# Grouping the up projection's matmuls by width, and starting stationary tiles at multiples of 64 bytes

## The chip, the cores and the metric

The kernel runs on one core of one Trainium2 chip. The metric is the device time of one execution in microseconds (us), median of several runs.

## The reference

A two-layer decoder trunk on a sequence of 256 tokens with a model width of 2048, all in float32. Layer 0 mixes tokens with a top-k latent attention and a sliding-window attention, layer 1 with a forgetting attention. After its mixer each layer does the same two things:

```python
x = x + conv_ffn(rms_norm(x, ffn_norm[i]), w_up[i], ffn_conv[i], w_down[i])
gate = jax.nn.sigmoid(rms_norm(x, ple_norm[i]) @ w_ple_gate[i])
x = x + gate * (p[i] @ w_ple_proj[i])

def conv_ffn(h, w_up, conv_w, w_down):
    u = h @ w_up                      # (256, 2048) @ (2048, 2 * 5504)
    u = causal depthwise conv of width 3 over the tokens (u, conv_w)
    gate, up = jnp.split(u, 2, axis=-1)
    return (jax.nn.silu(gate) * up) @ w_down   # (256, 5504) @ (5504, 2048)
```

The up projection `h @ w_up` is the place of the change.

## The kernel before, in words

**Precision.** Most products are made from float32 operands that are split in two float32r parts, a high part (a rounding copy) and a low part (what is left). A product is the sum of three: high by high, high by low, low by high.

**Weights.** `granule` (L105) hands out 128 rows by some columns of a weight matrix in several k tiles. One DMA on SP's queue brings 1 MB (as a rule) into a `raw` buffer (three of them, L100). Each half of it is then split: ScalarE casts it into a `whi` buffer (L114) and VectorE subtracts into a `wlo` buffer (L115). There are five `whi` and five `wlo` buffers, each for one half of a granule; a buffer comes free when the last matmul that reads it has run.

**The order of the work.** The program is written in one order, and a planner of the framework lays it out on the engines' queues with its own estimate of times. It can put an instruction ahead of earlier ones on the same queue; `tc.high_priority` moves whole sections forward.

**The up projection** (L821 to L838). The 43 blocks of 128 columns are done in two parts of 22 and 21, two blocks (z = 0, 1) at a time, once for the gate half and once for the up half (`base`). Each block accumulates in a PSUM bank of its own. For each of two granules of 8 k tiles (256 columns wide), and for each k, and for each z, two matmuls follow each other: the high part of the weights is stationary and both parts of `h` move past it (512 columns, L835), then the low part of the weights is stationary and the high part of `h` moves (256 columns, L837). Per layer that are 43 x 2 x 16 = 1376 such pairs, in both layers 2752, or 5504 matmuls; 88 granules a layer, 176 in all (168 of 1 MB; the last pass of the second part has one block alone, so that 8 are half as wide).

**Behind it.** ScalarE and VectorE take a finished bank, scale it, make the convolution and the gating (L842 to L856), and split the result into `ghi` and `glo` (L859, L860), one tile for each pass `f` in the part. Those tiles are stationary in **the down projection**, which follows each part (L866 to L869): for four times 512 columns, each k tile of the part is met three times in each half of the tokens (ghi with whi, ghi with wlo, glo with whi), all at 512 columns (L142). That are 43 x 3 x 2 x 4 = 1032 matmuls a layer, 2064 in all.

**Where tiles lie.** The pool `ff` of the feed-forward stage holds, in the order in which they are first asked for: `ghi0` and `glo0` (they serve the per-layer input first, as `pT_hi` and `pT_lo`), then `cw` with 3 x 86 float32 values, 1032 bytes in each partition, then `cr`, `rb`, `u`, `un`, `sg` and the other `ghi` and `glo`, each a multiple of 512 bytes. The allocator rounds a tile's size up to 32 bytes. In the program that results, `ghi0` and `glo0` begin at a multiple of 64 bytes, and every other `ghi` and `glo` begins 32 bytes past one. `whi`, `wlo` and the normed inputs (`nf`, `np`, `n`, `y`, `yc`) begin at a multiple of 64.

Of the kernel before, what the change touches and what calls it, by code (L numbers as in the profile page):

```python
# [9 lines left out]
F32 = mybir.dt.float32  # L10
# [6 lines left out]
P = 128  # L17
S = 256
# [7 lines left out]
H_C = 32  # L26
# [5 lines left out]
NFB = D_FF // P  # L32
PLE = 256
NB = 32
RV = 384
NEG = -1e30
MAXNEG = -3.0e38
CAUSAL = -1.0e37
PR = 300
HR = 6  # L40
UP_BANKS = ("mm", "qk")
MAGIC = float(0x5F3759DF)
# [4 lines left out]
def trunk(ctx, tc, t, onehot, out):  # L47
    nc = tc.nc
# [186 lines left out]
    def attention(pool, heads, b, qk, logits, vv, y_out, halves, extra=0, mask=None):  # L235

        nh = len(heads)
        n = P * (b + 1)
        nk = n // P
        o = psum("o")  # L240
        nl = sm.tile([P, 8], F32, tag="att_l", name="att_l", bufs=2)[:, :nh]
        rl = sm.tile([P, 8], F32, tag="att_r", name="att_r", bufs=2)[:, :nh]

        def front(grps):
            per = len(grps[0])
            pss = [psum("qk") for _ in grps]
            ss = [pool.tile([P, 516], F32, tag="att_s", name="att_s", bufs=4)[:, :per * (n + extra)]
                  .rearrange("p (h c) -> p h c", h=per) for _ in grps]

            for g, i, m in alternate(grps):  # L250
                pairs = qk(heads[m], b, n)
                for c, (lt, rh) in enumerate(pairs):
                    nc.tensor.matmul(pss[g][:, i * n:(i + 1) * n], lt, rh, start=c == 0, stop=c == len(pairs) - 1)  # L253
            for grp, ps, s in zip(grps, pss, ss):
                for i, m in enumerate(grp):
                    logits(s[:, i, :], ps[:, i * n:(i + 1) * n], heads[m], b, n)
                if mask is not None:
                    nc.vector.tensor_tensor(s[:, :, :n], s[:, :, :n], mask[:, None, :n].to_broadcast([P, per, n]), op=ALU.add)
                nm = sm.tile([P, 4], F32, tag="att_m", name="att_m", bufs=4)[:, :per]
                nc.vector.tensor_reduce(nm, s, axis=AX.X, op=ALU.max, negate=True)  # L260
                for i, m in enumerate(grp):
                    nc.scalar.activation(s[:, i, :], s[:, i, :], AF.Exp, bias=nm[:, i:i + 1],
                                         accum_out=nl[:, m:m + 1])
            lo, hi = min(min(g) for g in grps), max(max(g) for g in grps) + 1
            nc.vector.reciprocal(rl[:, lo:hi], nl[:, lo:hi])
            for grp, s in zip(grps, ss):
                for i, m in enumerate(grp):
                    nc.vector.tensor_scalar(s[:, i, :n], s[:, i, :n], rl[:, m:m + 1], None, op0=ALU.mult)
            return ss

        def back(grps, ss):
            per = len(grps[0])
            pTs = []
            for s in ss:
                pt = psum()
                for i in range(per):
                    for kb in range(nk):
                        nc.tensor.transpose(pt[:, (i * nk + kb) * P:(i * nk + kb + 1) * P],  # L278
                                            s[:, i, kb * P:(kb + 1) * P], ident)
                pT = pool.tile([P, 512], F32, tag="att_p", name="att_p", bufs=2)  # L280
                nc.scalar.copy(pT[:, :per * n], pt[:, :per * n])
                pTs.append(pT)

            at = {m: (g, i) for g, i, m in alternate(grps)}
            for m in sorted(at):
                if m % 2:
                    continue
                for kb in range(nk):
                    for mm in (m, m + 1):
                        g, i = at[mm]  # L290
                        z = (mm % 2) * HD
                        nc.tensor.matmul(o[z:z + HD, m // 2 * P:(m // 2 + 1) * P], vv(heads[mm], kb),  # L292
                                         pTs[g][:, (i * nk + kb) * P:(i * nk + kb + 1) * P],
                                         start=kb == 0, stop=kb == nk - 1, skip_group_check=True)

        prev = None
        for grps in head_groups(nh, n, halves):
            ss = front(grps)
            if prev is not None:
                back(*prev)  # L300
            prev = grps, ss
        back(*prev)
        nc.vector.tensor_copy(y_out, o[:, :nh * HD])
# [29 lines left out]
    def even_mixer(i, e):  # L333
        W = t["w_in_even"][e]
        with ExitStack() as es:
            ev = es.enter_context(tc.tile_pool(name="ev", bufs=1))
# [21 lines left out]
            h = norm(t["attn_norm"][i], "n0", gains)  # L358
# [10 lines left out]
            ss = sm.tile([P, NT, 1], F32, tag="ssq", name="ssq")  # L369
# [26 lines left out]
            for m in range(2):  # L396
                pr = psum()
                nc.tensor.matmul(pr[:16, :RV], tab[:, m * 16:(m + 1) * 16], oh[:, m, :], start=True, stop=True)
                rv = ev.tile([P, 516], F32, tag="att_s", name="rv", bufs=4)[:16, :RV]
                nc.scalar.copy(rv, pr[:16, :RV])  # L400
                nc.gpsimd.dma_start(rvd[m * 16:(m + 1) * 16, :], rv)


            qg_col = ev.tile([P, 2], F32, name="qg_col")
            nc.sync.dma_start(qg_col, t["a_q_norm"][e].rearrange("(k p) -> p k", p=P))
            kvT = ev.tile([P, 2, S], F32, name="kvT")
            kvgT = ev.tile([P, 2, S], F32, name="kvgT")
# [5 lines left out]
            ss = sm.tile([P, NT, 1], F32, tag="ssq", name="ssq")  # L413
# [30 lines left out]
            for c in range(2):  # L444
                hi, lo = granule(Wqi, 0, 4, c * 512, 512)
                for f in range(0, 4, 2):
                    pq = psum()
                    for ff in range(2):
                        cols = slice((f + ff) * P, (f + ff + 1) * P)
                        for k in range(4):  # L450
                            for m, (l, r) in enumerate(((hi, cq.hi), (hi, cq.lo), (lo, cq.hi))):
                                nc.tensor.matmul(pq[:, ff * S:(ff + 1) * S], l[k][:, cols], r[:, k, :],  # L452
                                                 start=k == 0 and m == 0, stop=k == 3 and m == 2)
# [24 lines left out]
            with tc.high_priority(offset=PR):  # L478
                for b in range(NT):
                    n = P * (b + 1)  # L480
# [5 lines left out]
                    for grps in head_groups(IDX_H, n, True):  # L486
                        pds = [psum("qk") for _ in grps]
                        for g, m, hh in alternate(grps):
                            q0 = (hh % 2) * HD
                            nc.tensor.matmul(pds[g][:, m * n:(m + 1) * n], qiT[hh // 8][q0:q0 + HD, (hh % 8) // 2, b * P:(b + 1) * P],  # L490
                                             kiT[q0:q0 + HD, :n], start=True, stop=True)
                        for grp, pd in zip(grps, pds):
                            rl = ev.tile([P, 516], F32, tag="att_s", name="relu", bufs=4)[:, :512]
                            nc.scalar.activation(rl, pd, AF.Relu)
                            for m, hh in enumerate(grp):
                                nc.vector.scalar_tensor_tensor(acc[:, :n], rl[:, m * n:(m + 1) * n],
                                                               wix[b][:, hh:hh + 1], acc[:, :n],
                                                               op0=ALU.mult, op1=ALU.add)
                    m8 = ev.tile([P, 8], F32, tag="m8", name="m8", bufs=2)
                    for _ in range(TOPK // 8):  # L500
                        nc.vector.max(m8, acc[:, :n])
                        nc.vector.match_replace(acc[:, :n], m8, acc[:, :n], MAXNEG)
# [4 lines left out]

            o5 = Q_LORA + KV_LORA + HD + IDX_H + H_B * HD
            ps = moving(W, o5, 4 * HD, h.lhs, KD)
            bg = ev.tile([P, 2], F32, name="bg")  # L510
            for m, nm in enumerate(("b_q_norm", "b_k_norm")):
                for z in range(2):
                    nc.sync.dma_start(bg[z * HD:(z + 1) * HD, m:m + 1], t[nm][e].rearrange("(d o) -> d o", o=1))
# [119 lines left out]
    def odd_mixer(i, o):  # L633
        W = t["w_in_odd"][o]
        HDC = H_C * HD
        with ExitStack() as es:
            od = es.enter_context(tc.tile_pool(name="od", bufs=1))
            h = norm(t["attn_norm"][i], "n1")
            rx = h.rstd
            cg = od.tile([P, 2], F32, name="cg")  # L640
            for m, nm in enumerate(("c_q_norm", "c_k_norm")):
                for zz in range(2):
                    nc.sync.dma_start(cg[zz * HD:(zz + 1) * HD, m:m + 1], t[nm][o].rearrange("(d o) -> d o", o=1))
# [70 lines left out]

            q0 = proj_q(0)

            fb = od.tile([H_C, 1], F32, name="fb")
            nc.sync.dma_start(fb, t["c_forget_bias"][o].rearrange("(d o) -> d o", o=1))
            hi, lo = granule(W, 0, KD, 3 * HDC, H_C)
            pf = psum()  # L720
# [80 lines left out]
    def ffn(i):  # L801
        with ExitStack() as es:
# [2 lines left out]
            with tc.high_priority(offset=PR):  # L805
                h = norm(t["ffn_norm"][i], "nf")

            cw = ff.tile([P, 3, 2 * NFB], F32, name="cw")
            cr = ff.tile([2 * NFB, 3, P], F32, name="cr")
            nc.sync.dma_start(cr, t["ffn_conv"][i].rearrange("w (f c) -> f w c", c=P))  # L810
            pt = psum()
# [8 lines left out]
            for part in parts:  # L820
                g_hi, g_lo = {}, {}  # L821
                f = 0
                while f < len(part):
# [3 lines left out]
                    for base in (0, NFB):  # L827

                        pu = [psum(next(up_banks)) for _ in range(nf)]
                        for k0 in (0, 8):  # L830
                            hi, lo = granule(t["w_up"][i], k0, 8, (base + fb0) * P, nf * P)
                            for k in range(8):
                                for z in range(nf):
                                    cols = slice(z * P, (z + 1) * P)
                                    nc.tensor.matmul(pu[z], hi[k][:, cols], h.both(k0 + k), start=k0 + k == 0,  # L835
                                                     stop=k0 + k == KD - 1, skip_group_check=True)
                                    nc.tensor.matmul(pu[z][:, :S], lo[k][:, cols], h.rhs(k0 + k)[0], start=False,  # L837
                                                     stop=k0 + k == KD - 1, skip_group_check=True)  # L838
                        u = ff.tile([P, 2, S], F32, tag="u", name="u", bufs=4)
                        un = ff.tile([P, 2, S], F32, tag="un", name="un", bufs=2)  # L840
# [106 lines left out]
```

## Time and profile before

| what | value |
|---|---|
| median of 3 runs | 2449.73 us (2448.8 to 2452.66) |
| the profiled execution | 2451.84 us, span 2450.1 us, mean granted clock 0.996 |
| TensorE matmul busy | 2426.1 us of the span, 12530 matmuls |
| TensorE weight loads | 2019.7 us |
| VectorE busy | 1687.4 us |
| ScalarE busy | 1266.4 us |
| DMA | 454.25 MB, mean 185 GB/s |

A share of busy time is an average over stages. For matmuls it says little of how near the engine is to its best, since matmuls are pipelined: a matmul's recorded length is longer than the distance from its start to the next one's start. What a matmul costs here is that distance.

### The profile page before, as it was taken

To read this page: it belongs to the slowest core of one execution; us is meant where nothing else is said; L and a number is where in the kernel's file an instruction comes from. 1 tells how busy PE (TensorE), PEld (TensorE's weight loads), DVE (VectorE), ACT (ScalarE), POOL (GpSimd) and SP (SyncE) were. 2 spreads that over 40 slices of the span, in tenths; PEclk is the share of its full clock that TensorE was granted. 3 is DMA by queue.
4 is the path that set the end of the run, shared out by engine and by line. 5 is a ranking of instruction groups with operands and counts; after the bars stand their busy time and mean duration, and the time that the engine had idled before them with its cause. 6 is when DMAs were issued, how large, how long until landed. Compare 5 with 4: busy or idle time off the path is not lost.

```text
span 2450.1 us, 32617 instructions
## 1 busy us (share of the span) xinstructions
PE 2426.1 (99%) x12530; PEld 2019.7 (82%) x12530; DVE 1687.4 (69%) x2670; ACT 1266.4 (52%) x1977; POOL 63.1 (3%) x138
## 2 busy tenths in 40 slices
PE   8999999999999999999999999999999999999999
PEld 6778788888888888888778777888888888888887
DVE  7777976777546777556676777677776457776564
ACT  6556655555335555444555555465554345554443
POOL 0000100000000000000030110000000000000000
PEclk9999999999999999999999999999999999999999
DMA  8444457555556655656565555475665566655564
GB/s 275 132 139 149 143 173 233 183 184 188 179 188 200 189 183 175 198 184 225 168 215 164 180 181 176 162 240 184 184 188 180 188 199 188 184 184 187 189 197 160
DMA packets 334000, 454.25 MB, mean 185 GB/s; under 512 B 15807, under 2 KB 210019, under 8 KB 333844
## 3 DMA queue, kind: packets, MB, share of 16 engines
q1 hardware_dynamic: 332468, 447.89, 57.4%
q0 software_dynamic: 1376, 4.28, 0.5%
q8 instruction: 98, 1.61, 0.3%
q14 instruction: 58, 0.48, 0.1%
HBM read 445.76 MB, written 6.37 MB: 185 GB/s over the span
## 4 chain that ended last, share of the span: by engine, by line
PE 90%; issue 7%; DVE 1%; DMA 1%; ACT 0%; POOL 0%; DVEq 0%; SPq 0%; POOLq 0%; ACTq 0%
PE ps_mm L142 44%; PE ps_mm L835 13%; PE ps_qk L835 13%; PE ps_mm L837 7%; PE ps_qk L837 7%; PE ps_qk L253 2%; PE ps_o L292 1%; PE ps_ax L278 1%; PE ps_ax L209 1%; PE ps_ax L169 1%; PE ps_ax L452 0%; DMA pled<-y 0%; PE ps_qk L490 0%; DMA gain<-in_attn_norm_dram 0%; DVE wlo L115 0%
## 5 line engine op out<-in xcount | busy, mean ns | idle before, releaser
L115 DVE TENSOR_TENSOR wlo<-raw,whi 128x1024 fp32r<-128x1024 f32 (+1 forms) x846 | 984.8, 1169 | 611.0 <-ACT whi L114 601.7
L114 ACT CAST whi<-raw 128x1024 fp32r<-128x1024 f32 (+1 forms) x846 | 848.4, 1006 | 855.3 <-PE ps_mm L142 514.0
L835 PE MATMUL ps_qk<-nf,whi 128*128 128x512 f32 x1376 | 546.9, 399 | 0.9 <-ACT whi L114 0.9
L835 PE MATMUL ps_mm<-nf,whi 128*128 128x512 f32 x1376 | 546.4, 399 | 0.4 <-ACT y L797 0.4
L837 PE MATMUL ps_qk<-nf,wlo 128*128 128x256 f32 x1376 | 386.9, 281 | 0.9 <-DVE wlo L115 0.9
L837 PE MATMUL ps_mm<-nf,wlo 128*128 128x256 f32 x1376 | 386.7, 281 | 0.0
L142 PE MATMUL ps_mm<-whi,n 128*128 128x512 f32 (+2 forms) x1088 | 335.9, 387 | 2.4 <-ACT n L121 1.9
L835 PEld LDWEIGHTS ps_qk<-nf,whi 128*128 128x128 f32 x1376 | 258.6, 188 | 65.5 <-ACT whi L114 1.6
L835 PEld LDWEIGHTS ps_mm<-nf,whi 128*128 128x128 f32 x1376 | 258.7, 188 | 65.2 <-ACT y L797 1.1
L142 PE MATMUL ps_mm<-whi,glo 128*128 128x512 f32 x688 | 272.2, 396 | 0.0
L142 PE MATMUL ps_mm<-wlo,ghi 128*128 128x512 f32 x688 | 271.7, 395 | 0.0
L142 PE MATMUL ps_mm<-whi,ghi 128*128 128x512 f32 x688 | 271.0, 396 | 0.0
L837 PEld LDWEIGHTS ps_qk<-nf,wlo 128*128 128x128 f32 x1376 | 260.1, 189 | 2.2 <-DVE wlo L115 1.9
L837 PEld LDWEIGHTS ps_mm<-nf,wlo 128*128 128x128 f32 x1376 | 260.0, 189 | 0.1
L142 PEld LDWEIGHTS ps_mm<-whi,n 128*128 128x128 f32 x1088 | 201.7, 190 | 46.1 <-issue 6.7
L142 PE MATMUL ps_mm<-wlo,n 128*128 128x512 f32 (+2 forms) x544 | 211.0, 389 | 0.0
L142 PE MATMUL ps_mm<-whi,np 128*128 128x512 f32 x512 | 158.7, 390 | 0.0
L142 PEld LDWEIGHTS ps_mm<-wlo,ghi 128*128 128x128 f32 x688 | 129.3, 188 | 31.0
L142 PEld LDWEIGHTS ps_mm<-whi,glo 128*128 128x128 f32 x688 | 129.3, 188 | 30.7
L142 PEld LDWEIGHTS ps_mm<-whi,ghi 128*128 128x128 f32 x688 | 129.0, 188 | 30.4
L142 PEld LDWEIGHTS ps_mm<-wlo,n 128*128 128x128 f32 x544 | 103.3, 190 | 20.4 <-issue 1.4
L142 PEld LDWEIGHTS ps_mm<-whi,np 128*128 128x128 f32 x512 | 96.0, 188 | 19.8
(215 smaller groups left out, 2470.0 us busy)
## 6 DMA issues: line engine op xcount, KB each, us to landing
raw<-in_w_up_dram SPq DMA_DIRECT2D x168, 1024.0 KB, 5.3
raw<-in_w_down_dram SPq DMA_DIRECT2D x80, 1024.0 KB, 5.1
raw<-in_w_in_odd_dram SPq DMA_DIRECT2D x48, 1024.0 KB, 5.1
raw<-in_w_ple_gate_dram SPq DMA_DIRECT2D x32, 1024.0 KB, 5.2
raw<-in_w_out_even_dram SPq DMA_DIRECT2D x16, 1024.0 KB, 5.1
raw<-in_w_out_odd_dram SPq DMA_DIRECT2D x16, 1024.0 KB, 5.1
raw<-in_a_w_uq_dram SPq DMA_DIRECT2D x8, 1024.0 KB, 5.4
raw<-in_w_in_even_dram SPq DMA_DIRECT2D x8, 1024.0 KB, 5.4
```

Source lines behind the costliest of these rows:

```text
L114: nc.scalar.copy(hi, v[:, z:z + m])
L115: nc.vector.tensor_tensor(lo, v[:, z:z + m], hi.bitcast(F32), op=ALU.subtract)
L142: nc.tensor.matmul(self.ps[b], l, r[i], start=self.n[b] == 0, stop=self.n[b] == 3 * self.total - 1)
L169: nc.tensor.transpose(pt[:, i * P:(i + 1) * P], src[:, i * P:(i + 1) * P], ident)
L209: nc.tensor.transpose(pt[:, i * parts:(i + 1) * parts], src[:, i * P:(i + 1) * P], ident[:parts, :parts])
L253: nc.tensor.matmul(pss[g][:, i * n:(i + 1) * n], lt, rh, start=c == 0, stop=c == len(pairs) - 1)
L278: nc.tensor.transpose(pt[:, (i * nk + kb) * P:(i * nk + kb + 1) * P], s[:, i, kb * P:(kb + 1) * P], ident)
L292: nc.tensor.matmul(o[z:z + HD, m // 2 * P:(m // 2 + 1) * P], vv(heads[mm], kb), pTs[g][:, (i * nk + kb) * P:(i * nk + kb + 1) * P], start= ...
L835: nc.tensor.matmul(pu[z], hi[k][:, cols], h.both(k0 + k), start=k0 + k == 0, stop=k0 + k == KD - 1, skip_group_check=True)
L837: nc.tensor.matmul(pu[z][:, :S], lo[k][:, cols], h.rhs(k0 + k)[0], start=False, stop=k0 + k == KD - 1, skip_group_check=True)
```

## The change

Two edits. In the up projection the loops inside a granule change places: first the high parts of all (z, k), z outside and k inside, then the low parts of all (z, k). The number of matmuls, weight loads, DMAs, casts and subtractions is the same. And tiles whose size is not a multiple of 64 bytes are asked for with a larger row and sliced, so that whatever is allocated behind them begins at a multiple of 64: `cw` in the feed-forward stage (1032 to 1152 bytes), `att_s`, `qg_col`, `m8`, `bg`, `cg` and `fb` in the mixers.

```diff
+CWB = 96
+ATW = 528
...
-            ss = [pool.tile([P, 516], F32, tag="att_s", name="att_s", bufs=4)[:, :per * (n + extra)]
+            ss = [pool.tile([P, ATW], F32, tag="att_s", name="att_s", bufs=4)[:, :per * (n + extra)]
...
-            qg_col = ev.tile([P, 2], F32, name="qg_col")
+            qg_col = ev.tile([P, 16], F32, name="qg_col")[:, :2]
...
-                    m8 = ev.tile([P, 8], F32, tag="m8", name="m8", bufs=2)
+                    m8 = ev.tile([P, 16], F32, tag="m8", name="m8", bufs=2)[:, :8]
...
-            cg = od.tile([P, 2], F32, name="cg")
+            cg = od.tile([P, 16], F32, name="cg")[:, :2]
...
-            cw = ff.tile([P, 3, 2 * NFB], F32, name="cw")
+            cw = ff.tile([P, 3, CWB], F32, name="cw")[:, :, :2 * NFB]
...
                             hi, lo = granule(t["w_up"][i], k0, 8, (base + fb0) * P, nf * P)
-                            for k in range(8):
-                                for z in range(nf):
-                                    cols = slice(z * P, (z + 1) * P)
-                                    nc.tensor.matmul(pu[z], hi[k][:, cols], h.both(k0 + k), start=k0 + k == 0,
+                            cols = [slice(z * P, (z + 1) * P) for z in range(nf)]
+
+                            for z in range(nf):
+                                for k in range(8):
+                                    nc.tensor.matmul(pu[z], hi[k][:, cols[z]], h.both(k0 + k), start=k0 + k == 0,
                                                      stop=k0 + k == KD - 1, skip_group_check=True)
-                                    nc.tensor.matmul(pu[z][:, :S], lo[k][:, cols], h.rhs(k0 + k)[0], start=False,
+                            for z in range(nf):
+                                for k in range(8):
+                                    nc.tensor.matmul(pu[z][:, :S], lo[k][:, cols[z]], h.rhs(k0 + k)[0], start=False,
                                                      stop=k0 + k == KD - 1, skip_group_check=True)
```

## Rows read from the trace of the kernel before

**Rows 1.** The page, part 1: busy time, share, instructions of each engine.
```profile
PE 2426.1 (99%) x12530; PEld 2019.7 (82%) x12530; DVE 1687.4 (69%) x2670; ACT 1266.4 (52%) x1977; POOL 63.1 (3%) x138
```

**Rows 2.** Windows: length, busy time (instructions) by engine, clock, DMA.
```profile
core 0: us, PE busy (x) PEld busy (x) DVE busy (x) ACT busy (x) POOL busy (x), PEclk, DMA share, GB/s
...
740.30:977.80 237.50, 237.50 (x1346) 206.15 (x1345) 176.93 (x252) 128.41 (x191) 0.00 (x0) 1.00 0.60 186
...
1999.20:2236.70 237.50, 237.50 (x1346) 206.04 (x1345) 176.93 (x252) 128.42 (x191) 0.00 (x0) 1.00 0.60 186
```

**Rows 3.** Timeline of TensorE's matmuls in the up projection: start, length, what.
```profile
900.39 0.28 PE L837 MATMUL ps_mm<-nf,wlo 128*128 128x256 f32 x1
900.51 0.40 PE L835 MATMUL ps_qk<-nf,whi 128*128 128x512 f32 x1
900.75 0.28 PE L837 MATMUL ps_qk<-nf,wlo 128*128 128x256 f32 x1
900.86 0.40 PE L835 MATMUL ps_mm<-nf,whi 128*128 128x512 f32 x1
901.10 0.28 PE L837 MATMUL ps_mm<-nf,wlo 128*128 128x256 f32 x1
```

**Rows 4.** Chain that ended last: start, length and count of its long pieces.
```profile
64.34 5.74 PE ps_ax L452 x48
...
1225.31 5.46 PE ps_ax L724 x48
...
1876.58 122.94 PE ps_mm L142 x528
2236.96 61.03 PE ps_mm L142 x262
...
2366.13 78.92 PE ps_mm L142 x348
```

**Rows 5.** Timeline of the matmuls of the single last block, one bank.
```profile
973.29 0.40 PE L835 MATMUL ps_qk<-nf,whi 128*128 128x512 f32 x1
973.53 0.28 PE L837 MATMUL ps_qk<-nf,wlo 128*128 128x256 f32 x1
...
975.41 0.40 PE L835 MATMUL ps_qk<-nf,whi 128*128 128x512 f32 x1
```

**Rows 6.** Timeline of down matmuls; those from 648.26 to 649.40 load ghi0, glo0.
```profile
647.10 0.40 PE L142 MATMUL ps_mm<-wlo,ghi 128*128 128x512 f32 x1
...
648.03 0.40 PE L142 MATMUL ps_mm<-whi,glo 128*128 128x512 f32 x1
...
648.49 0.39 PE L142 MATMUL ps_mm<-wlo,ghi 128*128 128x512 f32 x1
...
649.40 0.40 PE L142 MATMUL ps_mm<-whi,glo 128*128 128x512 f32 x1
```

**Rows 7.** Groups of matmuls by line and shape: transposes, whole span.
```profile
L169 PE MATMUL ps_ax<-ident,xg 128*128 128x128 f32 x192 | 29.5, 282 | 7.8 <-DVE xg L188 6.1 <-DVE rq_v L73 1.0 <-DVE n L122 0.7
L278 PE MATMUL ps_ax<-ident,att_s 128*128 128x128 f32 x192 | 27.3, 279 | 0.0
```

**Rows 8.** Waits, 740 to 980: who waited for whom, us, times, longest.
```profile
ACT whi L114 <- PE ps_qk L835: 67.8, 50, 1.8
DVE wlo L115 <- ACT whi L114: 50.0, 61, 2.1
```

**Rows 9.** Timeline where the up projection starts in each layer.
```profile
363.66 0.38 PE L837 MATMUL ps_qk<-nf,wlo 128*128 128x256 f32 x1 [0.30 <-DVE wlo L115]
...
1623.95 0.38 PE L837 MATMUL ps_qk<-nf,wlo 128*128 128x256 f32 x1 [0.57 <-DVE wlo L115]
```

**Rows 10.** Groups of weight loads by line and shape, whole span.
```profile
L837 PEld LDWEIGHTS ps_mm<-nf,wlo 128*128 128x128 f32 x1376 | 260.0, 189 | 0.1
...
L452 PEld LDWEIGHTS ps_ax<-cq_hi,whi 128*128 128x128 f32 x32 | 6.1, 191 | 0.2
```

**Rows 11.** Timeline of weight loads in the stretch of rows 3.
```profile
900.40 0.19 PEld L835 LDWEIGHTS ps_qk<-nf,whi 128*128 128x128 f32 x1
900.52 0.19 PEld L837 LDWEIGHTS ps_qk<-nf,wlo 128*128 128x128 f32 x1
900.75 0.19 PEld L835 LDWEIGHTS ps_mm<-nf,whi 128*128 128x128 f32 x1
```

**Rows 12.** DMA issues of the page: count, size, median us to landing.
```profile
raw<-in_w_up_dram SPq DMA_DIRECT2D x168, 1024.0 KB, 5.3
```

More of the change, by code (lines that the diff above doesn't have):

```diff
@@ L398, in even_mixer @@
                 nc.tensor.matmul(pr[:16, :RV], tab[:, m * 16:(m + 1) * 16], oh[:, m, :], start=True, stop=True)
-                rv = ev.tile([P, 516], F32, tag="att_s", name="rv", bufs=4)[:16, :RV]
+                rv = ev.tile([P, ATW], F32, tag="att_s", name="rv", bufs=4)[:16, :RV]
                 nc.scalar.copy(rv, pr[:16, :RV])
                 nc.gpsimd.dma_start(rvd[m * 16:(m + 1) * 16, :], rv)
-            qg_col = ev.tile([P, 2], F32, name="qg_col")
+            qg_col = ev.tile([P, 16], F32, name="qg_col")[:, :2]
             nc.sync.dma_start(qg_col, t["a_q_norm"][e].rearrange("(k p) -> p k", p=P))
@@ L492, in even_mixer @@
                         for grp, pd in zip(grps, pds):
-                            rl = ev.tile([P, 516], F32, tag="att_s", name="relu", bufs=4)[:, :512]
+                            rl = ev.tile([P, ATW], F32, tag="att_s", name="relu", bufs=4)[:, :512]
                             nc.scalar.activation(rl, pd, AF.Relu)
@@ L509, in even_mixer @@
             ps = moving(W, o5, 4 * HD, h.lhs, KD)
-            bg = ev.tile([P, 2], F32, name="bg")
+            bg = ev.tile([P, 16], F32, name="bg")[:, :2]
             for m, nm in enumerate(("b_q_norm", "b_k_norm")):
@@ L715, in odd_mixer @@
             q0 = proj_q(0)
-            fb = od.tile([H_C, 1], F32, name="fb")
+            fb = od.tile([H_C, 16], F32, name="fb")[:, :1]
             nc.sync.dma_start(fb, t["c_forget_bias"][o].rearrange("(d o) -> d o", o=1))
```

## The prediction

> **What bounds the kernel now.** I read the page's busy times first, then the windows by stage, then the timeline inside the stages that the change touches. TensorE's matmuls are busy for 2426.1 of 2450.1 us and no other engine is over 69% [rows 1]. That alone proves little, since recorded lengths overlap. The windows of the second part of the up projection say more: TensorE is busy all of the 237.50 us at the full granted clock (1.00, the 2.4 GHz level), while VectorE works 176.93 us (74%), ScalarE 128.41 us (54%) and the DMA engines 60% [rows 2]. And what the others wait for points at TensorE: ScalarE's casts waited 67.8 us for matmuls to give a `whi` buffer back, and VectorE waited for ScalarE behind them [rows 8]. The producers run as far ahead as five buffers let them. So here only the distance from one matmul's start to the next counts, and I price everything in that.
>
> **Distances now.** Part two of the up projection holds 21 x 2 x 16 = 672 pairs of a high and a low matmul; 237.50 us / 672 = 353.4 ns a pair [rows 2]. The timeline shows how a pair divides: a 512-column matmul starts, the 256-column one follows about 0.24 us later (900.51 to 900.75), and the next high one 0.11 to 0.12 us after that (900.39 to 900.51) [rows 3]. With no column lost a pair would take 768 columns / 2.4 GHz = 320 ns, so 33 ns are lost in each.
>
> Now streams of one width. `np` stationary, 512 columns all along: 78.92 us / 348 = 226.8 ns. A stationary `whi` or `wlo` with 256 columns moving, L452: 5.74 us / 48 = 119.6 ns [rows 4]. Each loses about 13 ns against its bare columns (213.3 and 106.7), so a high and a low matmul, each among its like, would take 226.8 + 119.6 = 346.4 ns, 7.0 less than in the mix. Is it the mix, or is it that two banks alternate? The last single block has one bank and the same alternation of widths: from 973.29 to 975.41 six pairs, 353 ns each [rows 5]. So banks are not it.
>
> The down projection, 512 columns all along, should then run at 226.8 too and doesn't: 122.94 us / 528 = 232.8 ns, and 61.03 / 262 = 232.9 [rows 4]. Inside the stage the distance changes with the stationary tile: among the matmuls that load `ghi0` and `glo0`, 648.49 to 649.40 are four steps, 0.91 us, 227 ns; a moment before, with other tiles, 647.10 to 648.03 are four steps, 0.93 us, 233 ns [rows 6]. The two kinds of tiles differ in nothing that I can see except that the first begin at a multiple of 64 bytes and the others 32 bytes past one.
>
> **The change part by part.** *Grouping.* The 5504 matmuls and their loads, 176 granules' DMAs, casts and subtractions all stay, on the same queues; nothing is moved past SP's or POOL's queue. What changes is who follows whom. 2752 pairs x 7.0 ns = 19.3 us. Each of the 176 granules still has one change of width each way, which I charge with the 7.0 ns of today's pair: 1.2 us back. Sum: -18.1 us. The 512-column half has no row of its own kind (stationary `whi`, 512 columns, among its like). Its bounds are 226.8 from `np` below and, above, what a high matmul takes now before its low one, 353.4 less the low one's 117 (the timeline's 0.11 to 0.12 us), 236 [rows 3]. For the low matmuls the nearest rows are 119.6 and, with a load of only 32 columns, 5.46 us / 48 = 113.8 (L724) [rows 4]. So a pair lies between 340.6 and 356: from -35 to +7 us over 2752. I take 226.8, as `np` is stationary and aligned as `whi` is, and 119.6, which is the same tiles and the same width.
>
> *Alignment in the feed-forward stage.* `cw` grows to 1152 bytes, 18 x 64, so all `ghi` and `glo` begin at a multiple of 64. Of 528 matmuls in part one, 2 of 22 k tiles (48 matmuls) are aligned already; the others take (122.94 - 48 x 0.2268) / 480 = 233.4 ns. In all 2064 x 39/43 = 1872 matmuls are off: x 6.6 ns = -12.4 us. Bounds: 0, and this.
>
> *Alignment in the mixers.* The attention's operands are plain float32. Transposes from `att_s`, half of whose buffers begin 32 bytes off, are no longer on record than those from `xg`, which begin on 64 (279 and 282 ns) [rows 7]. I take nothing. At the dearest, 6.6 ns on some 500 matmuls with such tiles gives -3.3 us.
>
> *When operands are needed.* At the start of each layer's up projection the first low matmul waits for its `wlo`, 0.30 and 0.57 us [rows 9]. It now comes 16 matmuls later: -0.9 us. The other side: z outside means that the second `whi` half of a granule is needed 4 x 226.8 = 0.9 us after the first, no longer 8 pairs or 2.8 us after. And `wlo`'s first half is given back after 16 high and 12 low matmuls, 5.1 us into a granule of 5.5 us, where it was 2.8. What is late next: VectorE's subtraction into that buffer, five halves on, which is for the second half of the granule after next, whose low matmuls read it 2 x 5.5 + 3.6 + 0.5 = 15.1 us after the first granule's start. 5.1 plus about 1.2 us of work leaves 8.8 us spare. Its `raw` buffer comes free some 2 us later than now; with 5.3 us from issue to landing [rows 12] the new data are there at about 5.1 + 1.2 + 5.3 = 11.6 us, and the first cast of them has no `whi` buffer before 14.7. ScalarE's queue holds the evictions of banks behind such casts; a finished `ps_qk` bank is wanted again only one base, 11 us, later. The cover is wide and I cost all this at nothing. Were it gone, each late second half could hold TensorE for up to 1.9 us (2.8 - 0.9) a granule.
>
> *Sum.* -18.1 - 12.4 - 0.9 = -31.4 us. The trace's execution took 2451.84 us (span 2450.1), the median is 2449.73; the differences are taken off the median: **2418 us**. For the likeliest case alone I give 2412 to 2426.
>
> **Where a page speaks against it.** The weight load's row of 188 ns is no distance: the load that starts at 900.40 feeds the matmul that starts at 900.51 [rows 3, 11]. The Trainium skill, "TensorE: Matmul & The Clock Gate", section "Back-to-back issue gap", gives the distance between matmuls as columns / 2.4 plus 2.5 ns, whatever came before. By that figure a pair would take an estimated 325 ns in either order. The trace disagrees on the size (353.4 mixed, 226.8 and 119.6 unmixed), but a rule without memory of the neighbour makes rival A below.
>
> On alignment, the rows above tell 227 from 233 ns at 0 and 32 bytes past 64. The Trainium skill, "SBUF — State Buffer", section "Door 1: The DMA port swizzle", speaks of lines of 16 bytes in that memory. By it a start 32 bytes off crosses no more lines than one at 64, and padding would bring nothing; that is rival B, and rows 6 are against it.
>
> **Rivals.**
> A. The order of widths changes nothing: a pair stays at 353.4 ns wherever it stands, for instance because `whi` under a moving `nf` costs this much by itself. For it: no row shows that pairing unmixed at 512. Against: L452 uses the same stationary tiles and shows 119.6. Time: 2449.7 - 12.4 = 2437. Chance 0.13.
> B. Alignment changes nothing, the tiles differ by something else. Against: rows 6. Time: 2449.7 - 18.1 - 0.9 = 2431. Chance 0.05.
> C. High matmuls keep today's 236 ns and low ones take 119.6: 355.6 a pair, 2752 x 2.2 = +6 us, with alignment 2449.7 + 6 - 12.4 = 2443. Chance 0.06.
> D. Slower: the low block, sixteen 256-column matmuls in a row, becomes bound by its weight loads, since each has to be loaded behind a matmul half as wide. If the recorded 189 ns [rows 10] were the distance, each low matmul would cost 69 ns more, 2752 x 69 = +190 us, 2608 us in all. It decides the sign from 119.6 + 31.4/2752 = 131 ns a low matmul on. Against: in L452's stream the load is recorded at 191 ns too, and the distance is 119.6 [rows 4, 10]. Chance 0.06.
> E. Both edits do nothing, 2449: chance 0.03.
> F. The unmixed streams are better than the rows, down to 340.6 a pair: 2449.7 - 35 - 12.4 - 0.9 = 2401. Chance 0.05.
> The likeliest case keeps 0.62.
>
> **How the numbers follow.** From 2410 to 2438 the range holds the likeliest case, A and B, 0.80, and leaves out C, D, E and F. About 0.2% (4.9 us) is what a measurement of this kernel can tell from no change. Faster by more than that are the likeliest, A, B, C and F, 0.91, from which I take 0.04 for planner's shifts in the mixers that no row prices: 0.87. Same: E and part of those shifts, 0.06. Slower: D and the rest, 0.07.
>
> **What would show it.** Right: in a granule sixteen 512-column matmuls about 0.227 us apart, then sixteen of 256 at about 0.12; part two of the up projection 233 us long, not 237.5; the down chain of 528 at 119.7 us, not 122.9; no wait of L835 on `whi` in the steady state. Wrong: high distances still at 0.236 (A or C), low ones over 0.131 (D), a down chain that stays at 122.9 (B), or a gap between a granule's fourth and fifth matmul.

## The result: faster by half of what was forecast

The changed kernel takes 2436.69 us (median of 4 runs, 2434.55 to 2437.99) against 2451.19 us of the kernel before (4 runs): a ratio of 0.9938, 95% interval 0.9919 to 0.9956, or 15 us less (11 to 20). Forecast were 2418 us and 31 us less. The span of the profiled execution went from 2450.1 to 2432.8 us. Lines have moved: the cast is L116, the split matmuls of `moving` are L144, the up projection's high and low matmuls are L839 and L843.

First the window of the second part of the up projection, from its first matmul to the down projection's first, in each layer (length, busy time and count by engine, clock, DMA):

```profile
core 0: us, PE busy (x) PEld busy (x) DVE busy (x) ACT busy (x) POOL busy (x), PEclk, DMA share, GB/s
734.84:968.65 233.81, 233.81 (x1346) 206.63 (x1345) 171.16 (x252) 125.40 (x191) 0.00 (x0) 1.00 0.60 189
1986.30:2220.11 233.81, 233.81 (x1345) 206.62 (x1345) 171.15 (x252) 125.35 (x191) 0.00 (x0) 1.00 0.61 189
```

233.81 us / 672 pairs are 347.9 ns a pair, where [rows 2] gave 353.4. The same stretch in the kernel before, cut at its first matmuls too, is 237.44 us:

```profile
1999.52:2236.96 237.44, 237.44 (x1346) 206.03 (x1345) 176.87 (x252) 128.36 (x192) 0.00 (x0) 1.00 0.60 186
```

The change takes 3.63 us from it, 5.4 ns a pair. Over 2752 pairs that makes 14.9 us, nearly all of the result.

The timeline there (start, length, what), whose merged rows begin where a block begins:

```profile
927.57 1.11 PE L843 MATMUL ps_mm<-nf,wlo 128*128 128x256 f32 x8
928.52 1.12 PE L843 MATMUL ps_qk<-nf,wlo 128*128 128x256 f32 x8
929.49 2.00 PE L839 MATMUL ps_mm<-nf,whi 128*128 128x512 f32 x8
931.33 1.98 PE L839 MATMUL ps_qk<-nf,whi 128*128 128x512 f32 x8
933.14 1.12 PE L843 MATMUL ps_mm<-nf,wlo 128*128 128x256 f32 x8
```

The grouping is there as written. The second eight high matmuls take 933.14 - 931.33 = 1.81 us, 226 ns each, as a stream of one width did in [rows 4]; the sixteen low ones 929.49 - 927.57 = 1.92 us, 120 each. But the first eight high ones, right behind the low block, take 1.84 us, 230 each: a change of width is paid for over several matmuls.

Then the long pieces of the chain that ended last (start, length, count):

```profile
612.22 122.62 PE ps_mm L144 x528
968.65 60.83 PE ps_mm L144 x262
...
2348.85 78.93 PE ps_mm L144 x348
```

This is where the forecast breaks. The down projection's 528 matmuls took 122.94 us [rows 4] and take 122.62, 232.2 ns each, where 119.7 us was expected; the 262 went from 61.03 to 60.83. `ghi` and `glo` all begin at a multiple of 64 bytes now, and the time from one matmul's start to the next hardly changes. The gate's 348 stay at 78.9 us.

The producers wait for TensorE as before; a buffer of `wlo` now comes back later, and VectorE waits for it, but no matmul of the up projection waits in this stretch (waits, 735 to 968: us, times, longest):

```profile
ACT whi L116 <- PE ps_qk L839: 98.7, 41, 3.6
DVE wlo L117 <- PE ps_qk L843: 46.4, 27, 3.2
```

### The profile page after: what moved, and what is told of

Read it like the earlier page. It is cut to its first block, busy times and chain, and to the rows that moved or that the text cites. A ratio compares the mean times of both kernels' runs of the same rounds, so it can differ in the third digit from the quotient of the medians.

```text
span 2432.8 us, 32646 instructions
## 1 busy us (share of the span) xinstructions
PE 2409.0 (99%) x12530; PEld 2022.7 (83%) x12530; DVE 1666.3 (68%) x2670; ACT 1253.0 (52%) x1977; POOL 62.5 (3%) x138
## 4 chain that ended last, share of the span: by engine, by line
PE 88%; issue 7%; DMA 2%; DVE 2%; ACT 0%; POOL 0%; SPq 0%; DVEq 0%; ACTq 0%; POOLq 0%
PE ps_mm L144 43%; PE ps_mm L839 13%; PE ps_qk L839 13%; PE ps_mm L843 7%; PE ps_qk L843 7%; PE ps_qk L255 2%; DMA raw<-in_w_in_even_dram 1%; PE ps_o L294 1%; PE ps_ax L280 1%; DMA pled<-y 1%; PE ps_ax L211 1%; DVE wlo L117 1%; PE ps_ax L171 1%; PE ps_ax L454 0%; PE ps_qk L492 0%
## 5 line engine op out<-in xcount | busy, mean ns | idle before, releaser
L116 ACT CAST whi<-raw 128x1024 fp32r<-128x1024 f32 (+1 forms) x846 | 835.5, 1005 | 947.3 <-PE ps_mm L144 507.8
L839 PE MATMUL ps_mm<-nf,whi 128*128 128x512 f32 x1376 | 345.0, 392 | 0.6 <-ACT y L799 0.6
L839 PE MATMUL ps_qk<-nf,whi 128*128 128x512 f32 x1376 | 341.7, 390 | 0.5 <-ACT whi L116 0.5
L144 PE MATMUL ps_mm<-whi,n 128*128 128x512 f32 (+2 forms) x1088 | 336.5, 388 | 2.3 <-ACT n L123 1.9
L839 PEld LDWEIGHTS ps_qk<-nf,whi 128*128 128x128 f32 x1376 | 257.5, 188 | 54.0 <-ACT whi L116 1.1
L839 PEld LDWEIGHTS ps_mm<-nf,whi 128*128 128x128 f32 x1376 | 247.6, 189 | 45.6 <-ACT y L799 1.2
L144 PE MATMUL ps_mm<-whi,glo 128*128 128x512 f32 x688 | 271.4, 395 | 0.0
L144 PE MATMUL ps_mm<-wlo,ghi 128*128 128x512 f32 x688 | 271.1, 395 | 0.0
L144 PE MATMUL ps_mm<-whi,ghi 128*128 128x512 f32 x688 | 270.6, 395 | 0.0
L144 PEld LDWEIGHTS ps_mm<-whi,n 128*128 128x128 f32 x1088 | 202.2, 190 | 46.2 <-issue 6.7
L144 PE MATMUL ps_mm<-wlo,n 128*128 128x512 f32 (+2 forms) x544 | 210.7, 388 | 0.3 <-DVE wlo L117 0.3
L843 PEld LDWEIGHTS ps_mm<-nf,wlo 128*128 128x128 f32 x1376 | 187.7, 190 | 13.4
L843 PE MATMUL ps_qk<-nf,wlo 128*128 128x256 f32 x1376 | 193.4, 283 | 0.0
L843 PE MATMUL ps_mm<-nf,wlo 128*128 128x256 f32 x1376 | 191.9, 282 | 0.0
L843 PEld LDWEIGHTS ps_qk<-nf,wlo 128*128 128x128 f32 x1376 | 178.2, 192 | 0.8
L144 PE MATMUL ps_mm<-whi,np 128*128 128x512 f32 x512 | 158.8, 390 | 0.0
L144 PEld LDWEIGHTS ps_mm<-whi,glo 128*128 128x128 f32 x688 | 129.6, 188 | 30.2
L144 PEld LDWEIGHTS ps_mm<-wlo,ghi 128*128 128x128 f32 x688 | 129.6, 188 | 30.0
L144 PEld LDWEIGHTS ps_mm<-whi,ghi 128*128 128x128 f32 x688 | 129.5, 188 | 29.5
L144 PEld LDWEIGHTS ps_mm<-wlo,n 128*128 128x128 f32 x544 | 103.2, 190 | 20.6 <-issue 1.4
L144 PEld LDWEIGHTS ps_mm<-whi,np 128*128 128x128 f32 x512 | 96.0, 188 | 19.7
```

The costliest lines, as they stand in the source:

```text
L116: nc.scalar.copy(hi, v[:, z:z + m])
L144: nc.tensor.matmul(self.ps[b], l, r[i], start=self.n[b] == 0, stop=self.n[b] == 3 * self.total - 1)
L839: nc.tensor.matmul(pu[z], hi[k][:, cols[z]], h.both(k0 + k), start=k0 + k == 0, stop=k0 + k == KD - 1, skip_group_check=True)
L843: nc.tensor.matmul(pu[z][:, :S], lo[k][:, cols[z]], h.rhs(k0 + k)[0], start=False, stop=k0 + k == KD - 1, skip_group_check=True)
```

## The experiments

Two questions: which edit brought the 15 us, and why were `ghi0` and `glo0` fast [rows 6] if not for the 64 bytes? Looking again at where the allocator puts tiles, the two kinds differ in a second thing. `whi` and `wlo`, the moving tiles, begin at 128 modulo 512. The start of the stationary tile less that of the moving one, modulo 512, is 256 for `ghi0` and `glo0` in all kernels but one, named below; for the others it was 288 before and is 384 after the change. For `np` over `whi`, and `whi` under `nf`, it is 0 or a whole number of 512. I call it the distance in place; it is counted in bytes, where the distance of two matmuls is a time.

**The edits alone.** The first kernel has the new loops and the old tiles, the second the new tiles and the old loops.

> The kernel before with the grouping of the widths alone; cw and the other tiles as before. Theory 1 (the gain of the change is the grouping's, the padding adds nothing): about 2436, part two of the up projection 234 us where the kernel before has 237.5, the down chain of 528 matmuls still 122.9 us. Theory 2 (each edit brings part of the gain): about 2440, with the down chain of the changed kernel, 122.6 us, better than here by more than 1 us.

> The changed kernel with the up projection's old loop order; all stationary tiles begin at multiples of 64 bytes. Theory 1: no change against before, 2449 to 2451, the up projection's second part 237.5 us. Theory 2: 2440 to 2445.

Grouping alone: 2437.85 us, ratio 0.9953 (0.994 to 0.9966). Padding alone: 2445.8, ratio 0.999 (0.9982 to 0.9999). Part two of the up projection, first with the grouping alone, then with the padding alone:

```profile
736.72:970.53 233.81, 233.81 (x1345) 206.60 (x1345) 171.28 (x252) 125.36 (x191) 0.00 (x0) 1.00 0.60 189
```

```profile
733.88:971.31 237.43, 237.43 (x1345) 205.91 (x1345) 176.96 (x252) 128.43 (x192) 0.00 (x0) 1.00 0.59 186
```

The chain's long pieces, grouping alone:

```profile
613.75 122.96 PE ps_mm L142 x528
970.53 61.07 PE ps_mm L142 x262
```

and padding alone:

```profile
611.27 122.60 PE ps_mm L144 x528
971.31 60.83 PE ps_mm L144 x262
```

Nearly all of the gain is the grouping's: it alone brings 0.5%, and all that the up projection's second part gains. The padding takes 0.3 us from a chain of 123 and 0.1% from the whole. Theory 1 holds but for this 0.1%.

**The distance in place.** Only the length of `cw` changes, which shifts every tile behind it:

```diff
-            cw = ff.tile([P, 3, CWB], F32, name="cw")[:, :, :2 * NFB]
+            cw = ff.tile([P, 320], F32, name="cw")[:, :6 * NFB].rearrange("p (w f) -> p w f", w=3)
```

with 320 for a distance of 0, 384 for 256, 336 for 64 and 368 for 192. `ghi` and `glo` begin at a multiple of 64 bytes in all four.

> The changed kernel with 128 bytes more in cw, so that all ghi and glo but the first pair begin at the same place modulo 512 bytes as the moving whi and wlo (distance 0, where the changed kernel has 384 and the one before 288). Theory A (what counts is the distance of the stationary tile's start from the moving tile's, modulo 256 or 512; 0 and 256 are good): the down chain of 528 falls from 122.6 to 119.8 us, all in all 12 us less than the changed kernel, about 2424. Theory B (the first pair was fast for another reason than its address): the chain stays at 122.6 and the time at 2436.

> As the run before it, with the distance 256 bytes, where the first pair ghi0 and glo0 lies in every kernel. Theory A with modulo 256: the down chain falls to 119.8 us as at distance 0, about 2424. Theory A with modulo 512 (only 0 is good): between 119.8 and 122.6. Theory B: 122.6, about 2436.

Distance 0: 2424.53 us, ratio 0.9897 (0.9884 to 0.991). Distance 256: 2422.04, ratio 0.989 (0.9878 to 0.9903). The chain's long pieces at 0:

```profile
611.12 119.71 PE ps_mm L144 x528
964.64 59.42 PE ps_mm L144 x262
```

and at 256:

```profile
611.02 119.71 PE ps_mm L144 x528
964.54 59.42 PE ps_mm L144 x262
```

119.71 us / 528 = 226.7 ns: the down projection now runs as fast as the gate, and the 12 us that the forecast had put down to the 64 bytes are there. Theory A, modulo 256.

> The changed kernel with all ghi and glo but the first pair 64 bytes past the moving whi and wlo, counted modulo 256. They begin at a multiple of 64 bytes as the change wants it. Theory A (distance from the moving tile modulo 256 must be 0): the down chain of 528 stays slow, 122 to 123 us, about 233 ns a matmul. Rival (a multiple of 64 is enough and the changed kernel's 384 is a special case): 119.7 us.

> The same with 192 bytes modulo 256. Theory A: the down chain stays slow, 122 to 123 us. Rival: 119.7 us.

One run each, 2438.0 and 2426.82 us, so that the chains carry the argument and not the totals. The chain at 64:

```profile
612.98 123.09 PE ps_mm L144 x528
```

and at 192:

```profile
610.89 120.77 PE ps_mm L144 x528
```

At 64 the chain is as slow as ever, 233.1 ns, though the tiles begin at a multiple of 64: the rival falls. At 192 I was wrong: 228.7 ns, most of the way to the good value. So the loss is no matter of yes and no. By distance modulo 256, chain by 528: 0, 226.7 ns; 32 (before), 232.8; 64, 233.1; 128 (changed kernel), 232.2; 192, 228.7. Each of these means has the 48 matmuls of `ghi0` and `glo0`, at 256, in it.

**Is it the tile's own place or the distance?** Two pads of 128 bytes in the changed kernel. The first stands ahead of the weights' pool and shifts everything together; the second between the weights and the normed inputs, and shifts `n`, `nf`, `np`, `y`, `yc` against the weights, and with them all that lies behind.

```diff
     xs = [[xt[j][:, b, :] for j in range(4)] for b in range(NT)]
+    const.tile([P, 32], F32, name="cpad")
```

```diff
+    gp.tile([P, 32], F32, tag="gpad", name="gpad")
     ahead = {}
```

> The changed kernel with a pad of 128 bytes ahead of the weights' pool, so that whi, wlo, nf, np, ghi and glo all begin 128 bytes later and keep their distances; ghi now begins at 128 modulo 512, where it was fast in the run with distance 0. If the distance counts: nothing moves, down chain 122.6, gate chain of 348 78.9 us, part two of the up projection 234 us. If the stationary tile's own place counts (128 modulo 256 is good): down chain 119.7, gate chain about 81 us.

> The changed kernel with a pad of 128 bytes between the weights' pool and the pool of the normed inputs: nf, np, n, y and yc now begin 128 bytes off whi and wlo modulo 256, and ghi and glo at distance 0. If the distance counts wherever such matmuls are: down chain 119.7 us, but the gate chain of 348 goes from 78.9 to about 80.8 us, and the high blocks of the up projection from 226.7 to about 232 ns a matmul, 6 to 8 us more over the two layers' up projections; the mixers' projections lose too, so that the sum is 2436 or more. If it is a matter of ghi and glo alone: gate and up stay, and the time is about 2424.

One run each again: 2433.62 and 2449.44 us. The chain with all shifted:

```profile
613.38 122.62 PE ps_mm L145 x528
...
1098.55 78.93 PE ps_mm L145 x348
```

and with the normed inputs shifted against the weights:

```profile
618.22 120.03 PE ps_mm L145 x528
...
1101.04 80.86 PE ps_mm L145 x348
```

Shifted together nothing moves, though `ghi` lies at 128 modulo 512, where it was fast at distance 0. Shifted apart, down and gate change places: the gate's stationary `np`, now 128 off, goes from 226.8 to 80.86 / 348 = 232.4 ns, and the down chain falls. It stops at 120.03 and not at 119.71 since the first pair is now 128 off: 48 matmuls x 6 ns = 0.3 us. The up projection loses too. Its second part in that run:

```profile
738.24:974.40 236.16, 236.16 (x1346) 206.22 (x1345) 171.46 (x252) 125.79 (x191) 0.00 (x0) 1.00 0.60 187
```

2.35 us more than the changed kernel's 233.81, with the same order; over all 2752 pairs that would be 9.6 us, a little over the 6 to 8 expected. One granule of it on the chain (start, length, count):

```profile
811.34 1.86 PE ps_mm L840 x8
813.20 1.86 PE ps_qk L840 x8
815.06 0.94 PE ps_mm L844 x8
816.00 0.95 PE ps_qk L844 x8
```

The sixteen high matmuls take 3.72 us, where the changed kernel has 1.84 + 1.81 = 3.65; the sixteen low ones 1.89, where it has 1.92. So it is the distance in place, and it holds for `ghi`, `glo`, `np` and `whi` as stationary tiles at 512 columns. At 256 columns, with the same 128 bytes between the tiles, nothing is lost. The run with this one pad took 16 us more than the run with all shifted and 13 more than the changed kernel's median, though the pad mended the down projection.

**The price of a change of width.** Two kernels on the one with distance 256: groups of half a granule, and an order in which every second granule begins with its low matmuls.

```diff
+                            for kk in (0, 4):
-                                for k in range(8):
+                                    for k in range(kk, kk + 4):
```

```diff
+                            for part_of in (high, low) if k0 == 0 else (low, high):
+                                part_of()
```

> The kernel with ghi at 256, grouping inside half a granule instead of a whole one: eight high, then eight low matmuls, so twice as many changes of width. Theory M (each change of width there and back costs about 24 ns, as the changed kernel's part two shows: 234.0 us less 672 x 346.7 ns, over 42 full granules and 2 half ones): part two of the up projection 235.0 us, 4 us more in all than the run with ghi at 256, about 2426. Rival (a change costs the 7 ns that it costs when every pair changes): 234.3 us, 1 us more in all.

> The kernel with ghi at 256, where every second granule of a block does its low matmuls first, so that two high blocks follow each other from granule to granule and there are half as many changes of width. Theory M: part two 233.5 us instead of 234.0, about 2 us less in all than the run with ghi at 256, 2420 to 2422. Rival (low matmuls first need the subtraction's result at the start of a granule, and TensorE waits for it): waits of the low matmuls' line on wlo, and 2424 or more.

Half groups: 2426.67 us, ratio 0.992 (0.9905 to 0.9934). Alternate order: 2424.14, ratio 0.9912 (0.9897 to 0.9927). Part two with half groups:

```profile
733.34:968.02 234.68, 234.68 (x1346) 206.47 (x1345) 174.88 (x253) 128.48 (x191) 0.00 (x0) 1.00 0.61 189
```

and in the alternate order:

```profile
733.74:967.14 233.40, 233.40 (x1345) 206.73 (x1345) 170.65 (x251) 124.45 (x191) 0.00 (x0) 1.00 0.61 189
```

Without any change, 672 pairs of 226.7 + 120 ns are 232.98 us. Whole groups lose 0.83 us over 44 granules, 19 ns for each change there and back; half groups lose 0.87 us more, 20 ns for each one added. The 24 ns of the expectation came from a window cut 0.2 us too long; the 7 ns of the rival are out. Half as many changes give back 0.41 us in part two, as theory M has it, but under 2 us in the whole, which the medians do not show: the interval of this kernel and that of the one with distance 256 overlap. The median is the rival's 2424, but not for its reason: one low matmul waited for `wlo`, 0.3 us early in the first layer, and none in part two.

**The gains add.** The kernel before, in its old order, with `cw` at 384 floats and nothing else:

> The kernel before, in its old order, with cw at 1536 bytes, so that ghi and glo lie 256 bytes off the moving tile modulo 512; no other edit. If the two gains add: down chain 119.7 us, up part two 237.5, about 2436 to 2437. If the down projection's gain needs the grouping: more.

2434.32 us, ratio 0.9943 (0.9926 to 0.996), the chain:

```profile
618.32 119.74 PE ps_mm L142 x528
975.49 59.40 PE ps_mm L142 x262
```

Part two of the up projection stays at 237.43 us, as expected of the old order. One tile's length alone is worth as much as the whole change. The ratios of the two edits alone, 0.9953 and 0.9943, multiply to 0.9896, and both together measured 0.989. The best versions are the changed kernel with distance 256 (0.989 of the kernel before) and with distance 0 (0.9897), whose intervals overlap.

## Why the prediction was wrong, step by step

**What bounds the kernel** was right where the change acts: TensorE is not short of operands in the up projection's second part, and what the eleven runs gain and lose there, in the down projection and in the gate is the time between starts. At the start of each layer's up projection TensorE does wait for operands, once for 2.8 us in the run with half groups; that blurs the totals by a few us.

**Grouping** had the right mechanism and too large a size. Forecast -18.1 us, measured -14.9 (part two's rows over all pairs). The unmixed pair is 346.7 ns, 0.3 more than taken (0.8 us over all pairs). The change of width costs 19 ns a granule and not the 7 of a mixed pair: 176 x 12 = 2.1 us. Taking today's price of a pair for it was the mistake. That the 7 ns come of prices that run into each other, where every pair changes, is a guess that no run tests.

**Alignment in the feed-forward stage** is the step that failed: "so all `ghi` and `glo` begin at a multiple of 64 ... x 6.6 ns = -12.4 us". Measured: 0.32 us on the chain of 528 and 0.20 on 262 of 504, about 1.4 us in the two layers. The rows were right, 227 and 233 ns in one stage by tile; the reading was not. "The two kinds of tiles differ in nothing that I can see" overlooked that they also differ in their distance from the moving tile, and the padding took that from 288 to 384, one bad value to another. The chain of [rows 4] could not tell the two readings apart: `np` and `whi` agree with either, since they too are at a multiple of 64 and at distance 0.

**The mixers** at nothing: the padding alone gave 0.1% in all, of which the down projection has half. **When operands are needed**: no wait of the high matmuls came up in the steady state, as said. In the first layer the wait of 0.30 us [rows 9] is gone, but in its place the broadcast of `rstd` (L204) waits 0.21 us for the last normed input; in the second layer it waits 0.54. Of the 0.9 us little is left.

**The rivals.** A, that the order does nothing, is out (0.9953 for the order alone), although its time, 2437, is the one that came: the right number for the wrong reason. B, that alignment does nothing, named the failing step with 2431 and a chance of 0.05; it was given too little, because two values of one property were taken for a proof of it. C and D did not come: high blocks run at 226 to 230 ns and low ones at 120.

On the pages cited there: the Trainium skill, "TensorE: Matmul & The Clock Gate", section "Back-to-back issue gap", gives columns / 2.4 plus 2.5 ns as the gap of isolated matmuls, a condition that the prediction left out. No stream here runs at it: they take 226.7 and 120.0 ns. On the other page the runs cut both ways. By the lines of 16 bytes in the Trainium skill, "SBUF — State Buffer", section "Door 1: The DMA port swizzle", the padding has nothing to gain; the padding alone gained 0.1%. But by those lines there is no loss at 32 or 64 bytes either, and the runs at 0 and 256 gained 12 us on tiles that begin on such lines in all kernels.

**Open.** Why a distance of 32, 64 or 128 modulo 256 costs 5 to 6 ns at 512 columns, 192 only 2, and 128 nothing at 256 columns, is not settled. The period of 256 bytes rests on two agreements: 0 with 256 in the down projection, and 384 there (232.2 ns) with 128 at the gate (232.4). The load of the next stationary tile runs while the present matmul's operand moves [rows 3, 11], so that two streams read the same memory side by side; that they hinder each other when their addresses stand badly is an argument that fits, not one that these runs show. Nor is it shown why a change of width is paid for over several matmuls.

## What to carry to other kernels

Where TensorE is the bound, price matmuls by the time from start to start in a stretch that nothing else disturbs, and compare it by tile: 6 ns in 230 made 12 us here. When two groups of rows differ, list every property in which they differ before one of them is made the cause, and move that one alone. And after any edit that moves tiles, compare the distances in place of stationary and moving tiles modulo 256 bytes: a pad of 128 bytes cost 13 to 16 us in one run of this kernel, and one tile's length was worth 12.

## What the runs showed of the hardware

With 128 x 128 float32r stationary tiles at the full granted clock, matmuls follow each other in 226.7 ns at 512 columns and 120.0 ns at 256, in a stream of one width and with stationary and moving tiles at a distance of 0 modulo 256 bytes. At the other distances tried 512 columns take 228.7 to 233.1 ns (means of a chain); 256 columns lost nothing at 128 bytes, the only other distance at which such float32r tiles met them. Alternating the two widths costs 6.6 ns a pair, and a change there and back between longer blocks 19 to 20 ns.
